# Sixteen gate tiles through seven-product units, weight sums by accumulating DMA, stores on SyncE

## The chip, the core and the metric

The kernel runs on one core of one Trainium2 chip. What counts is the device time of one execution in microseconds (us); lower is better. TensorE (PE) multiplies, VectorE (DVE) and ScalarE (ACT) work on tiles, GpSimd (POOL) and SyncE (SP) issue transfers here, and POOL does a few small operations too.

## The reference, cut to what matters

One residual block over 1024 tokens of width 1024, in float32:

```python
h   = rmsnorm(x, ln_mix)
z   = h @ w_in                      # q | k | v | g | pool channels u | gate_logits (2 x 1024)
y_ret  = (silu(g) * groupnorm(retention(q, k, v))) @ w_ret_up
y_pool = (multiscale_pool(u, pool_w) * pool_scale) @ w_pool_up
gates  = sigmoid(gate_logits + b_gate)
x   = x + (gates[..., :D] * y_ret + gates[..., D:] * y_pool) @ w_o
x   = x + square(relu(rmsnorm(x, ln_mlp) @ w_up)) @ w_down
out = rmsnorm(x, ln_final)
```

The change is about `gate_logits`, a 1024 x 1024 by 1024 x 2048 product, and about how the weights of `h2 @ w_up` are prepared.

## The kernel before

**Products.** A float32 operand is held as a pair of rounded halves, hi and lo, and each product is three passes (hi hi, hi lo, lo hi). The hi part is made by ACT (line 132), the lo part by DVE (line 133): that is `split_pair`. Everything is feature-major: a tile is 128 features by 1024 tokens, in two halves of 512 tokens, and a matmul has 128 x 128 stationary weights and 512 moving columns. A full tile, `feature_major`, has 8 blocks of the inner dimension x 3 passes x 2 halves = 48 matmuls.

**Stages.** q, k, v and the retention by heads; the swish gates `ps_g` (8 tiles); then 8 times a gate tile `ps_ga` and a tile of the retention's up-projection `ps_yr`; the pool channels; the gate tiles `ps_gb` (8 tiles); the pool's up-projection `ps_yp`; `ps_o`; then the MLP, `up` and down. Sixteen gate tiles take 16 x 48 = 768 matmuls. All of that stays in SBUF; only `x1` and the MLP's activations go to DRAM.

**Seven-product units.** The MLP's up-projection is done by a scheme of the Strassen-Winograd kind. A unit j takes a 2 x 2 block of weights (two feature tiles by two halves of the inner dimension: a11, a12, a21, a22) and the 2 x 2 blocks of the moving operand, and does seven block products of 12 matmuls each instead of eight: 84 matmuls for two feature tiles. It needs four sums of weight blocks, s1 = a21 + a22, s2 = s1 + a11, s3 = a11 + a21, s4 = a12 + s2. DVE adds them (lines 620, 621, 631 and 636), and all seven stationary operands are then split. The sums of the moving blocks (T1 to T4) are made once, in `moving_operands`.

**Buffers and queues.** The tag `w` has four buffers of 8 KB per partition: in the up stage each unit takes two of them, `raw` for its four weight blocks and `sums` for the four sums. The four output tiles of a unit, `o[0]` to `o[3]`, have one buffer each, since the moving operands fill the rest of tags `r` and `h`: the next unit cannot write its outputs before the store of the last ones has landed. SP issues the loads; POOL issues the stores of `x1` and of the activations. The order of instructions on each engine is set when the program is built, by a scheduler with a model of the engines; on the chip each queue then runs in that order, and an instruction whose wait isn't over holds up all that stand behind it on its queue.

Of the kernel before, what the change touches and what calls it, by code (L numbers as in the profile page):

```python
# [10 lines left out]
F32 = mybir.dt.float32  # L11
# [27 lines left out]
def block_kernel(ctx: ExitStack, tc: tile.TileContext, a: dict, out: bass.AP):  # L39
# [116 lines left out]
    def token_rstd(sums, name):  # L156
# [11 lines left out]
        return spread(rstd_of(ssq, name, n), n, name)  # L168

# [226 lines left out]
    retT = []  # L396
    for f in range(KT):
        w = load_piece(a["w_fm"][8 + f], f"w_g{f}")
        r = retn[f]
        pairs = []  # L400
        for half in range(2):
            sl = slice(half * HALF, (half + 1) * HALF)
            ps = mm_bank(f"ps_g{f}_{half}")
            feature_major(ps, w, hT, half)
            sig = mm_bank(f"sig{f}_{half}")
            nc.vector.tensor_tensor(ps, ps, R1[:, sl], ALU.mult)
            nc.scalar.activation(sig, ps, AF.Sigmoid)
            nc.vector.scalar_tensor_tensor(
                r[:, sl], r[:, sl], vec[:, V_GNG + f : V_GNG + f + 1], sig, ALU.mult, ALU.mult
            )  # L410
            nc.vector.tensor_tensor(r[:, sl], r[:, sl], ps, ALU.mult)
            dst = pair_tile("r", f"retT{f}_{half}")
            split_pair(dst, r[:, sl])
            pairs.append(dst)
        retT.append(pairs)


    mixed = []
    for f in range(KT):
        w = load_piece(a["w_fm"][20 + f], f"w_ga{f}")  # L420
        m = a_tile("a", f"m{f}")
        for half in range(2):
            sl = slice(half * HALF, (half + 1) * HALF)
            ps = mm_bank(f"ps_ga{f}_{half}")
            feature_major(ps, w, hT, half)
            nc.vector.tensor_tensor(ps, ps, R1[:, sl], ALU.mult)
            nc.scalar.activation(
                m[:, sl], ps, AF.Sigmoid,
                bias=vec[:, V_BG + f : V_BG + f + 1],
            )  # L430
        w = load_piece(a["w_ret"][f], f"w_ret{f}")
        for half in range(2):
            sl = slice(half * HALF, (half + 1) * HALF)
            ps = mm_bank(f"ps_yr{f}_{half}")
            feature_major(ps, w, retT, half)
            nc.vector.tensor_tensor(m[:, sl], m[:, sl], ps, ALU.mult)
        mixed.append(m)


# [3 lines left out]
    ypT = []  # L443
    pooled = []
    for g, win in enumerate(WINDOWS):
# [22 lines left out]
    sgB = []  # L468
    for f in range(KT):
        w = load_piece(a["w_fm"][28 + f], f"w_gb{f}")  # L470
        s = a_tile("r", f"sgB{f}")
        for half in range(2):
            sl = slice(half * HALF, (half + 1) * HALF)
            ps = mm_bank(f"ps_gb{f}_{half}")
            feature_major(ps, w, hT, half)
            nc.vector.tensor_tensor(ps, ps, R1[:, sl], ALU.mult)
            nc.scalar.activation(
                s[:, sl], ps, AF.Sigmoid,
                bias=vec[:, V_BG + KT + f : V_BG + KT + f + 1],
            )  # L480
        sgB.append(s)
        if f < 4:
            pairs = []
            for half in range(2):
                ps = aux_bank(f"ps_pw{f}_{half}")
                exact(
                    ps,
                    lambda s: pw[:, s, f * P : (f + 1) * P],
                    lambda s: pooled[f][half][:, s, :],
                )  # L490
                dst = pair_tile("r", f"ypT{f}_{half}")
                split_scaled(dst, ps, vec[:, V_PSC + f : V_PSC + f + 1])
                pairs.append(dst)
            ypT.append(pairs)


    mixT = []
    for f in range(KT):
        if f % 2 == 0:
            w = load_piece(a["w_pool"][f // 2], f"w_po{f}", cols=256)  # L500
        pairs = []
        for half in range(2):
            sl = slice(half * HALF, (half + 1) * HALF)
            ps = mm_bank(f"ps_yp{f}_{half}")
            feature_major(ps, w, ypT, half, nk=4, j0=(f % 2) * P)
            s, m = sgB[f], mixed[f]
            nc.vector.tensor_tensor(s[:, sl], s[:, sl], ps, ALU.mult)
            nc.vector.tensor_tensor(m[:, sl], m[:, sl], s[:, sl], ALU.add)
# [6 lines left out]
    dram = ctx.enter_context(tc.tile_pool(name="dram", bufs=1, space=bass.MemoryType.DRAM))  # L515
    x1_dram = dram.tile([KT, P, S], F32, name="x1_dram")
    act_dram = [dram.tile([NJ, P, 2, HALF], F32, name=f"act_dram{i}") for i in range(3)]
    act_dram.append(dram.tile([NJ, P, HALF], F32, name="act_dram3"))
# [11 lines left out]
    B11, B21, B22, T1, T2, T3, T4 = range(7)  # L530
# [21 lines left out]
    for k in range(4):  # L552
# [20 lines left out]
        for f in (k, k + 4):  # L573
            nc.gpsimd.dma_start(x1_dram[f], x1[f])
# [7 lines left out]
    def up(j):  # L582
        raw = w_tile(f"raw_up{j}", F32)
        nc.sync.dma_start(raw, a["w_up"][j])
        raw = raw.rearrange("p (b j) -> p b j", b=4)
        a11, a12, a22, a21 = (raw[:, i, :] for i in range(4))
# [327 lines left out]
```

## Time and profile before

| what | value |
|---|---|
| median of 3 runs | 1421.11 us (1419.1 to 1422.63) |
| profiled execution, its own time | 1419.43 us |
| its span, first to last instruction | 1417.7 us |
| PE busy | 1385.3 us, 98% of the span, 6656 matmuls |
| DVE busy | 891.6 us, 63% |
| ACT busy | 502.4 us, 35% |
| POOL busy | 65.6 us, 5% |
| DMA | 183.11 MB, 129 GB/s in the mean |

A busy share is an average over stages; what a stage is worth is read from its own stretch of the span. The view by windows gives for each stretch the busy time of each engine, the granted TensorE clock (1.00 is full), the share of the 16 DMA engines' time that was busy, and GB/s. The chain of waits follows the work that ended last back to its start, and names the engine that it was on at each step.

### The profile page before, as it was taken

The page shows a single profiled execution, that of the slowest core. Times are in us where ns is not written, and L with a number is a line of the kernel's source. Part 1 is how long each engine was busy: PE and PEld are TensorE (multiplying, and loading weights), DVE is VectorE, ACT ScalarE, POOL GpSimd, SP SyncE. Part 2 cuts the span into 40 slices and gives each one's busy share as a digit, 9 for nine tenths or more (in the row PEclk, how much of TensorE's full clock was granted, in tenths as well). Part 3 has the DMA queues.
Part 4 walks back from the last instruction along what each step waited for, and adds up shares of the span by engine and source line. Part 5 has one row for each costly group of instructions (what it writes and reads, how often), then busy time and mean ns, then how long its engine had stood idle before and what let it go on. Part 6 is the DMA issues. An engine that isn't in the chain of part 4 may idle for free.

```text
span 1417.7 us, 17117 instructions
## 1 busy us (share of the span) xinstructions
PE 1385.3 (98%) x6656; PEld 1162.8 (82%) x6656; DVE 891.6 (63%) x1461; ACT 502.4 (35%) x832; POOL 65.6 (5%) x107
## 2 busy tenths in 40 slices
PE   9999999999999999999999999999998999999985
PEld 6998999888888888888887788888887888878874
DVE  5766667763222246327558788777777867669593
ACT  6232324432111112223345343333333544435272
POOL 0000000000000000000000111110111000000001
PEclk9999999999999999999999999999999999999998
DMA  9112011012111211113322244434459977739251
GB/s 350 48 57 60 31 31 44 32 45 60 45 45 45 67 45 45 45 45 119 134 74 104 90 163 157 157 133 149 164 218 385 402 252 240 244 138 371 94 178 60
DMA packets 56209, 183.11 MB, mean 129 GB/s; under 512 B 6528, under 2 KB 8576, under 8 KB 54080
## 3 DMA queue, kind: packets, MB, share of 16 engines
q1 hardware_dynamic: 45408, 143.98, 29.4%
q0 software_dynamic: 10576, 38.02, 7.1%
q8 instruction: 52, 0.85, 0.2%
q14 instruction: 29, 0.24, 0.1%
q10 hardware_dynamic: 144, 0.03, 0.0%
HBM read 144.24 MB, written 37.75 MB: 128 GB/s over the span
## 4 chain that ended last, share of the span: by engine, by line
PE 94%; DVE 2%; issue 2%; ACT 1%; DMA 0%; POOL 0%; POOLq 0%; SPq 0%; DVEq 0%; ACTq 0%
PE ps_v L119 6%; PE ps_g L119 6%; PE ps_o L119 6%; PE ps_gb L119 6%; PE ps_yr L119 6%; PE ps_ga L119 6%; PE ps_dnX L716 6%; PE ps_upZ L598 6%; PE ps_upV L598 6%; PE ps_upX L598 6%; PE ps_dnV L716 6%; PE ps_dnZ L716 5%; PE ps_qT L119 3%; PE ps_kT L119 3%; PE ps_upY L598 3%; PE ps_dnY L716 3%
## 5 line engine op out<-in xcount | busy, mean ns | idle before, releaser
L716 PE MATMUL ps_dnX<-db,da 128*128 128x512 f32 x384 | 94.1, 394 | 4.3 <-ACT db L132 4.3
L119 PE MATMUL ps_v<-w_v_hi,hT 128*128 128x256 f32 x512 | 95.9, 284 | 0.0
L598 PE MATMUL ps_upX<-mv,a_up 128*128 128x512 f32 x384 | 94.2, 390 | 1.7 <-DVE a_up L133 1.6
L598 PE MATMUL ps_upZ<-mv,s_up 128*128 128x512 f32 x384 | 93.1, 390 | 0.3 <-ACT s_up L132 0.3
L119 PE MATMUL ps_g<-hT,w_g 128*128 128x512 f32 x384 | 90.2, 391 | 0.0
L716 PEld LDWEIGHTS ps_dnX<-db,da 128*128 128x128 f32 x384 | 73.0, 191 | 20.2 <-ACT db L132 4.7
L119 PE MATMUL ps_ga<-hT,w_ga 128*128 128x512 f32 x384 | 88.3, 389 | 0.0
L119 PE MATMUL ps_yr<-retT,w_ret 128*128 128x512 f32 x384 | 88.3, 389 | 0.0
L119 PE MATMUL ps_gb<-hT,w_gb 128*128 128x512 f32 x384 | 87.8, 389 | 0.0
L119 PE MATMUL ps_o<-mixT,w_o 128*128 128x512 f32 x384 | 87.5, 389 | 0.0
L598 PEld LDWEIGHTS ps_upX<-mv,a_up 128*128 128x128 f32 x384 | 71.9, 188 | 17.3 <-DVE a_up L133 2.0
L598 PEld LDWEIGHTS ps_upZ<-mv,s_up 128*128 128x128 f32 x384 | 71.9, 188 | 15.9 <-ACT s_up L132 1.1
L119 PEld LDWEIGHTS ps_ga<-hT,w_ga 128*128 128x128 f32 x384 | 72.1, 188 | 15.0
L119 PEld LDWEIGHTS ps_yr<-retT,w_ret 128*128 128x128 f32 x384 | 72.1, 188 | 15.0
L119 PEld LDWEIGHTS ps_gb<-hT,w_gb 128*128 128x128 f32 x384 | 72.1, 188 | 15.0
L119 PEld LDWEIGHTS ps_o<-mixT,w_o 128*128 128x128 f32 x384 | 72.0, 188 | 14.9
L119 PEld LDWEIGHTS ps_g<-hT,w_g 128*128 128x128 f32 x384 | 71.3, 188 | 14.2
L119 PEld LDWEIGHTS ps_v<-w_v_hi,hT 128*128 128x128 f32 x512 | 80.8, 192 | 0.0
L119 PE MATMUL ps_v<-w_v_lo,hT 128*128 128x256 f32 x256 | 72.7, 284 | 0.0
L613 ACT ACTIVATE act<-act 128x512 f32<-128x512 f32 x64 | 40.4, 632 | 69.0 <-DVE act L612 66.2
L132 ACT ACTIVATE s_up<-sum_up 128x512 fp32r<-128x512 f32 x64 | 39.9, 629 | 64.8 <-PE ps_upZ L598 24.7
L119 PE MATMUL ps_qT<-hT,w_qT 128*128 128x512 f32 x192 | 49.9, 407 | 1.8 <-ACT hT L136 1.5
(231 smaller groups left out, 2621.2 us busy)
## 6 DMA issues: line engine op xcount, KB each, us to landing
act_dram<-act POOLq DMA_DIRECT2D x48, 512.0 KB, 3.6
ad<-act_dram SPq DMA_DIRECT2D x48, 512.0 KB, 6.0
raw_up<-in_w_up_dram SPq DMA_DIRECT2D x16, 1024.0 KB, 4.9
wa_lo<-in_w_down_dram SPq DMA_DIRECT2D x16, 512.0 KB, 9.0
wb_hi<-in_w_down_dram SPq DMA_DIRECT2D x16, 512.0 KB, 4.1
wc_lo<-in_w_down_dram SPq DMA_DIRECT2D x16, 512.0 KB, 5.2
wc_hi<-in_w_down_dram SPq DMA_DIRECT2D x16, 512.0 KB, 5.8
xT<-in_xT_dram SPq DMA_DIRECT2D x8, 512.0 KB, 9.4
```

Source lines behind the costliest of these rows:

```text
L119: nc.tensor.matmul(ps, stationary(k, sa), moving(k, sb), start=i == 0, stop=i == n - 1)
L132: nc.scalar.activation(dst[:, 0, :], src, AF.Copy)
L598: nc.tensor.matmul(ps, w[:, sa, k * P : (k + 1) * P], h2[x][k][:, sb, :], start=start and k == 0 and n == 0, stop=k == 3 and n == 2, skip_ ...
L613: nc.scalar.activation(dst, dst, AF.Square)
L716: nc.tensor.matmul(banks[i][:, c0 : c0 + n], w[:, sa, i * P : (i + 1) * P], x[:, sb, c0 : c0 + n], start=start and j == 0 and m == 0, stop ...
```

## The change

Three things are done together.

1. The sixteen gate tiles go through eight units of seven products (`gates`), which share the code with the up-projection (`seven`). The moving blocks of the normalised input that the units need (T1 to T4) are made from a second load of x (`mixed_blocks`). Because these take 16 buffers of tag `r`, the retention output, the pool output and the sigmoids no longer stay in SBUF: each is stored to DRAM and loaded again. The order of stages becomes swish with the pool in between, gates, `ps_yp`, `ps_yr`, `ps_o`.
2. The sums of weight blocks are no longer added by DVE, in the gate units and in the up units alike. SP loads `raw` with three blocks (768 KB) and fills all four blocks of `sums` with a21 (1024 KB, one block read four times); then three accumulating transfers from POOL's queue add a22 to s1, s2 and s4 (768 KB), a11 to s2, s4 and s3 (768 KB), and a12 to s4 (256 KB). They write the same tile, so each waits until the one before it has landed.
3. The stores of `x1` and of the activations move from POOL's queue to SP's, among the loads.

```diff
+    def seven(name, src, moving, done):
+        src = src.rearrange("p (b j) -> p b j", b=4)
+        raw = w_tile(f"raw_{name}", F32).rearrange("p (b j) -> p b j", b=4)
+        nc.sync.dma_start(raw[:, :3, :], src[:, :3, :])
+        a11, a12, a22 = (raw[:, i, :] for i in range(3))
+        sums = w_tile(f"sum_{name}", F32).rearrange("p (b j) -> p b j", b=4)
+        s1, s2, s4, s3 = (sums[:, i, :] for i in range(4))
+        nc.sync.dma_start(sums, src[:, 3:, :].to_broadcast([P, 4, HALF]))
+        for b, i0, i1 in ((2, 0, 3), (0, 1, 4), (1, 2, 3)):
+            nc.gpsimd.dma_start(
+                sums[:, i0:i1, :], src[:, b : b + 1, :].to_broadcast([P, i1 - i0, HALF]),
+                accum_op=ALU.add,
+            )
+
+        def mult(ps, src, x, start=True):
+            w = pair_tile("a", f"w{x}_{name}")
+            split_pair(w, src)
...
+        mult(X, a11, B11)
+        nc.scalar.activation(p1, X, AF.Copy)
+        mult(Y, s2, T2)
+        nc.vector.tensor_tensor(u2, p1, Y, ALU.subtract)
+        mult(X, a12, B21, start=False)
+        done(0, 0, X)
+        mult(Z, s1, T1)
+        nc.vector.tensor_tensor(u4, u2, Z, ALU.add)
+        mult(V, s3, T3)
+        done(1, 1, V, u4)
+        mult(Z, s4, B22, start=False)
+        done(0, 1, Z, u2)
+        mult(V, a22, T4, start=False)
+        done(1, 0, V, u2)
...
-        w = load_piece(a["w_fm"][20 + f], f"w_ga{f}")
-        m = a_tile("a", f"m{f}")
-        for half in range(2):
-            sl = slice(half * HALF, (half + 1) * HALF)
-            ps = mm_bank(f"ps_ga{f}_{half}")
-            feature_major(ps, w, hT, half)
-            nc.vector.tensor_tensor(ps, ps, R1[:, sl], ALU.mult)
...
+    def mixed_blocks(k):
+        xw = w_tile(f"xw{k}", F32).rearrange("p (i t) -> p i t", i=2)
+        nc.gpsimd.dma_start(xw, a["xT"].rearrange("(i k p) t -> k p i t", i=2, p=P)[k])
...
+            nc.vector.tensor_tensor(dst, x, y, op)
+            hx[t][k] = pair_tile("r", f"hx{t}_{k}")
+            split_pair(hx[t][k], dst)
...
+    def gates(i):
...
+            nc.vector.tensor_tensor(y, y, R1[:, sl], ALU.mult)
+            nc.scalar.activation(
+                dst, y, AF.Sigmoid, scale=-1.0 if m else 1.0,
+                bias=vec[:, V_BG + f : V_BG + f + 1],
+            )
+            left[m] -= 1
+            if not left[m]:
+                nc.sync.dma_start(sg_dram[f], o[m])
+
+        seven(f"sg{i}", a["w_gate"][i], hx, done)
...
-            nc.gpsimd.dma_start(x1_dram[f], x1[f])
+            nc.sync.dma_start(x1_dram[f], x1[f])
...
-        nc.vector.tensor_tensor(s1, a21, a22, ALU.add)
-        nc.vector.tensor_tensor(s2, s1, a11, ALU.add)
...
-        nc.gpsimd.dma_start(act_dram[0][j], o[0])
-        nc.gpsimd.dma_start(act_dram[2][j], o[2])
...
+                nc.sync.dma_start(act_dram[0][j], o[0])
+                nc.sync.dma_start(act_dram[2][j], o[2])
```

**How the order moves, on POOL.** In the middle of the up stage POOL's queue held the four stores of each unit (units 6 and 7; `act3_6` is the output tile 3 of unit 6):

```order
L651 DMA act_dram1_5139<-act1_6_6694 128x1024
L645 DMA act_dram2_5140<-act2_6_6695 128x1024
L644 DMA act_dram0_5138<-act0_6_6693 128x1024
L652 DMA act_dram3_5141<-act3_6_6696 128x512
L651 DMA act_dram1_5139<-act1_7_6838 128x1024
```

It now holds nothing but the accumulating transfers, unit after unit (two of 768 KB, one of 256 KB):

```order
L187 DMA sum_up13_7977<-in_w_up_dram 128x512
L187 DMA sum_up14_8121<-in_w_up_dram 128x3x512 x2
L187 DMA sum_up14_8121<-in_w_up_dram 128x512
L187 DMA sum_up15_8265<-in_w_up_dram 128x3x512 x2
L187 DMA sum_up15_8265<-in_w_up_dram 128x512
```

The transfers of one unit stand in a chain on a queue that runs in order, so the sums of unit 15 cannot begin before the last of unit 14 has been issued.

**On SP.** Before, the up stage's part of SP's queue was one load per unit, and the unit's number is all that differs:

```order
L584 DMA raw_up8_6976<-in_w_up_dram 128x2048
L584 DMA raw_up9_7120<-in_w_up_dram 128x2048
L584 DMA raw_up10_7264<-in_w_up_dram 128x2048
L584 DMA raw_up11_7408<-in_w_up_dram 128x2048
L584 DMA raw_up12_7552<-in_w_up_dram 128x2048
```

Now two loads and four stores alternate:

```order
L181 DMA raw_up9_7399<-in_w_up_dram 128x1536
L185 DMA sum_up9_7401<-in_w_up_dram 128x4x512
L713 DMA act_dram2_5415<-act2_6_6965 128x1024
L712 DMA act_dram0_5413<-act0_6_6963 128x1024
L716 DMA act_dram1_5414<-act1_6_6964 128x1024
L717 DMA act_dram3_5416<-act3_6_6966 128x512
L181 DMA raw_up10_7543<-in_w_up_dram 128x1536
L185 DMA sum_up10_7545<-in_w_up_dram 128x4x512
```

The loads of unit 9 need the two `w` buffers of unit 7, and the stores of unit 6 stand behind them.

**On DVE.** The additions are gone, and the splits of unit 9 (`w4` is s2, `w3` is s1, `w5` is s3, `w2` is s4) stand among the evacuations of unit 8. Before, at the same place for units 11 to 14, the sums were added nearly three units ahead of their use:

```order
L620 TENSOR_TENSOR sum_up14_7842<-raw_up14_7840 128x512
L631 TENSOR_TENSOR sum_up14_7842<-raw_up14_7840 128x512
L648 TENSOR_TENSOR act1_11_7414<-tmp_up11_7411,ps_upV11_7420 128x512
L621 TENSOR_TENSOR sum_up14_7842<-sum_up14_7842,raw_up14_7840 128x512
L641 TENSOR_TENSOR act1_11_7414<-act0_11_7413,act2_11_7415 128x512
L133 TENSOR_TENSOR a11_up13_7709<-raw_up13_7696,a11_up13_7709 128x512
```

Now:

```order
L133 TENSOR_TENSOR w4_up9_7428<-sum_up9_7401,w4_up9_7428 128x512
L715 TENSOR_TENSOR act3_7_7110<-act0_7_7107,act1_7_7108 128x512
L211 TENSOR_TENSOR tmp_up8_7262<-tmp_up8_7262,ps_Yup8_7265 128x512
L133 TENSOR_TENSOR w1_up9_7444<-raw_up9_7399,w1_up9_7444 128x512
L215 TENSOR_TENSOR u4_up8_7263<-tmp_up8_7262,ps_Zup8_7266 128x512
L133 TENSOR_TENSOR w3_up9_7461<-sum_up9_7401,w3_up9_7461 128x512
```

The split of s2 of unit 9 stands ahead of the reading of the bank Y of unit 8: if the sums of unit 9 are late by then, DVE stops, and the banks of unit 8 are not read.

More of the change, by code (lines that the diff above doesn't have):

```diff
@@ L442, in block_kernel, with pool @@
     split_pair(pw, pw_raw)
[L443 removed]
+    yp_dram = dram_tile("yp_dram", (4, P, S))
     pooled = []
[L445 removed]
+    def pool(g):
+        win = WINDOWS[g]
         w = load_piece(a["w_fm"][16 + g], f"w_pu{g}")
@@ L498, in block_kernel @@
+    for i in range(KT):
+        gates(i)
+    ypT = []
+    for f in range(4):
+        y = a_tile("a", f"ypf{f}")
+        nc.sync.dma_start(y, yp_dram[f])
+        ypT.append([])
+        for half in range(2):
+            dst = pair_tile("h", f"ypT{f}_{half}")
+            split_pair(dst, y[:, half * HALF : (half + 1) * HALF])
+            ypT[f].append(dst)
+    mixed = []
     for f in range(KT):
```

245 lines of the change are left out of this document (125 added, 120 removed).

## The prediction

> **What bounds the kernel now.** I read the page first (span, busy times, the chain of waits by engine), then the windows by stage, then the chain in order of time.
>
> ```profile
> span 1417.7 us, 17117 instructions
> PE 1385.3 (98%) x6656; PEld 1162.8 (82%) x6656; DVE 891.6 (63%) x1461; ACT 502.4 (35%) x832; POOL 65.6 (5%) x107
> PE 94%; DVE 2%; issue 2%; ACT 1%; DMA 0%; POOL 0%; POOLq 0%; SPq 0%; DVEq 0%; ACTq 0%
> ```
>
> The chain that ended last lies on PE for 94%. By stage (columns: window, length, then busy time and count for PE, PEld, DVE, ACT, POOL, then the granted clock, the share of the DMA engines, GB/s):
>
> ```profile
> 278.00:500.00 222.00, 222.00 (x981) 183.82 (x980) 74.44 (x92) 43.89 (x58) 0.77 (x1) 1.00 0.16 49
> 545.00:637.00 92.00, 92.00 (x408) 76.17 (x407) 33.39 (x43) 23.44 (x33) 0.00 (x0) 1.00 0.14 46
> 762.00:805.00 43.00, 39.03 (x176) 30.84 (x175) 36.70 (x61) 20.69 (x36) 5.36 (x4) 1.00 0.28 98
> 805.00:1060.00 255.00, 255.00 (x1127) 211.22 (x1126) 199.26 (x323) 98.36 (x162) 29.98 (x56) 1.00 0.44 163
> 1060.00:1084.00 24.00, 19.71 (x88) 16.02 (x87) 13.96 (x23) 5.43 (x9) 4.00 (x8) 1.00 0.98 358
> 1100.00:1125.00 25.00, 25.00 (x112) 20.68 (x111) 22.95 (x39) 14.51 (x26) 0.00 (x0) 1.00 1.03 404
> 1125.00:1225.00 100.00, 100.00 (x443) 82.80 (x442) 69.28 (x111) 44.00 (x78) 0.00 (x0) 1.00 0.77 259
> ```
>
> In the gate stages (rows 1 and 2) and in the up stage (row 4) PE is never idle. The idle time lies at the start of the up stage (row 3, 4.0 us) and at its end (row 5, 4.3 us). So a matmul taken away is worth its whole time there, and a DVE instruction taken away is worth nothing. The reader should also see the DMA column: 0.14 to 0.16 in the gate stages, 0.44 in the up stage, and at most 1.03, which moved 404 GB/s.
>
> **The matmuls removed.** The chain in order of time gives their pace (start, length, what):
>
> ```profile
> 348.82 10.88 PE ps_ga L119 x48
> 593.62 43.52 PE ps_gb L119 x192
> 899.99 2.72 PE ps_upV L598 x12
> ```
>
> 48 matmuls in 10.88 us are 226.7 ns each, the same in all three rows; a block product of 12 is 2.72 us. Sixteen gate tiles of 48 matmuls become eight units of 84: 768 - 672 = 96 fewer, 96 x 226.7 ns = **21.8 us**. This is the only gain on the path. The up stage keeps its 84 per unit, 7 x 2.72 = 19.04 us.
>
> **DVE and ACT.**
>
> ```profile
> L426 DVE TENSOR_TENSOR ps_ga<-ps_ga,R x16: 699/700/700, 332.5 to 490.3; 128x512 f32<-128x512 f32 x16
> L133 DVE TENSOR_TENSOR s_up<-sum_up,s_up x64: 679/683/694, 771.8 to 1055.7; 128x512 fp32r<-128x512 f32 x64
> L132 ACT ACTIVATE s_up<-sum_up x64: 614/632/636, 767.4 to 1055.1; 128x512 fp32r<-128x512 f32 x64
> ```
>
> A gate unit has seven splits, three additions and four multiplications by R1 on DVE: 14 x 0.69 = 9.7 us in 19.04; ACT has seven hi parts, a copy and four sigmoids, 12 x 0.65 = 7.8 us. An up unit loses four additions, 2.7 us of DVE, which lie beside a PE that is busy throughout: nothing. The moving blocks for the gates cost 4 x 8 x 0.69 = 22 us of DVE during swish and pool. These stages have 12 tiles of 10.88 us, 131 us in all; their DVE work was 72 us in the 105 us around swish (with the end of the retention) and 31 us in the 50 us around the pool (rows below), and about 11 us of retention splits leave: 114 in 131 or more, a share of 0.87 at worst. The up stage ran at 199/255 = 0.78 without a gap, so I put 1 us on it and no more.
>
> ```profile
> 225.00:330.00 105.00, 105.00 (x526) 89.02 (x525) 71.92 (x126) 40.74 (x68) 2.19 (x2) 1.00 0.14 46
> ...
> 500.00:525.00 25.00, 25.00 (x112) 20.68 (x111) 11.11 (x16) 4.34 (x5) 0.00 (x0) 1.00 0.14 43
> 525.00:550.00 25.00, 25.00 (x112) 20.70 (x111) 19.72 (x29) 4.44 (x6) 0.00 (x0) 1.00 0.20 59
> ```
>
> **The accumulating transfers** decide the rest, and the trace before has none. The rows that come nearest (operations x count, KB each, median us from issue to landing):
>
> ```profile
> raw_up<-in_w_up_dram SPq DMA_DIRECT2D x16, 1024.0 KB, 4.9
> pw_raw<-in_pool_w_dram POOLq DMA_DIRECT2D x1, 256.0 KB, 3.2
> act_dram<-act POOLq DMA_DIRECT2D x48, 512.0 KB, 3.6
> raw_w_ga<-in_w_fm_dram SPq DMA_DIRECT2D x8, 512.0 KB, 3.5
> wc_hi<-in_w_down_dram SPq DMA_DIRECT2D x16, 512.0 KB, 5.8
> ```
>
> From 256 KB at 3.2 to 1024 KB at 4.9 a further 768 KB costs 1.7 us, and what is fixed is 3.2 - 0.6 = 2.6. Three estimates for a unit's chain of 768, 768 and 256 KB, each after the landing of the last:
> - as plain loads: 4.3 + 4.3 + 3.2 = 11.8 us;
> - the data counted twice (source and destination are both read), the fixed part once: 6.0 + 6.0 + 3.8 = 15.8;
> - as two whole transfers, a read and a write: 23.6.
>
> POOL's queue takes the chains one after another, so a chain longer than 19.04 us sets the pace instead of PE. The first two are shorter, the third is not. I take the middle one: the sum must have both operands, and within one transfer the fixed part need not be paid twice.
>
> Then contention. An up unit moved 1024 KB in and 1792 KB out; it will load 768 + 1024, accumulate 1792 and store 1792: 5376 KB, 5.5 MB. At the up row's 163 GB/s for a share of 0.44, 5.5 MB in 19.04 us (289 GB/s) is a share of 0.78, and with the accumulated data counted twice 385 GB/s, or 1.04: just what the fullest row showed. In the row with 0.77 the 512 KB load `wc_hi` landed in 5.8 us against 3.5 for `raw_w_ga` at 0.16. The plain traffic of a unit, 3584 KB at 2.3 us per MB above the fixed part, is 8 us; the chain leaves 3 x 2.6 = 7.8 us in which it moves no data itself. If 40% of the plain traffic still falls into the chain's data, it is 15.8 + 3.2 = **19.0 us**: it just fits. Bounds: 11.8 if plain and unhindered, 23.6 + 8 = 32 at worst. In a gate unit the stores are 1024 KB, so the chain is nearer to 18.5.
>
> The sentence for the skill: the Trainium skill, "Collectives: The Full Stack", section "The bandwidth ceiling: the fold count and why AG ≠ RS ≠ AR", says that an adding transfer costs two source reads on the same ring and so moves at half the rate; no run so far shows it here, and by it the chain is at least the middle estimate. The Trainium skill, "DMA: Bandwidth & Descriptors", section "Anatomy of one DMA — SWDGE (gpsimd) path", gives about 2.0 us plus bytes at 436 GB/s, an estimate of 10.2 us for the chain, by which the whole 21.8 us would stay; its 2.6 us for 256 KB is under the measured 3.2.
>
> **Slack.** The loads for unit j+3 go out when the last split of unit j+1 frees its buffer, some 15 us into unit j. Before, SP waited in the same manner:
>
> ```profile
> SPq L584 <- DVE s_up L133: 250.5, 14, 20.1
> ```
>
> They land about 6.6 us later (4.9 for the first MB, 1.7 for the next 768 KB), two accumulations follow (12 us), so s2 is there 34 us after the start of unit j. DVE splits it ahead of the bank Y of unit j+2, which it can read as late as 6 us into that unit, 44 us after the start of unit j. So 10 us of lateness can be used up in each stage before PE waits, and a chain of 19.5 us costs nothing over 16 units. At the start of each stage there is less: the second unit's sums can only be loaded when the last `w_o` buffers come free, at the end of `ps_o`. That start cost 4.0 us before, on R2 and the first splits; I put 3 us more on the two starts together, and 1 us on the reloads of the pool and retention outputs at the end of the gates, which have the 43.5 us of `ps_yp` to arrive in.
>
> **The stores on SP** stand behind loads that wait. The outputs have one buffer each, and the wait for a store is already there:
>
> ```profile
>   DVE act L634: 4.2, 2
> ```
>
> 4.2 us in 2 waits (of all that waited for the stores of the activations). While the splits are early, SP's wait is over before the stores are ready, and a store from SP costs what one from POOL did (3.6 us to landing, above): nothing. If SP's loads come late, the stores do too.
>
> **Sum.** 1419.4 (the profiled execution: span 1417.7 and 1.7 around it) - 21.8 + 1 + 3 + 1 = 1402.6. That execution is 1.7 under the median of the runs, so the median should be **1404 us**.
>
> **Rivals.**
> 1. *The chain overruns and sets the pace.* One mechanism: POOL's queue, three serial transfers per unit, in the up stage above all. For it: 1.04 of the DMA engines with data counted twice, and `wc_hi` at 5.8 us. Against: the fixed parts leave room. At 22 us a chain: up 16 x 3.0 - 10 = 37, gates 8 x 2 - 10 = 6, so 1404 + 43 = 1447. It decides from 20.9 us on: 16 x 1.9 - 10 = 20, which with the starts eats the gain. The skill's rule of two reads, cited above, points this way.
> 2. *A draw*: the chain at 20.5 (1.5 x 16 - 10 = 14), or stores that SP holds back by 1 us in each of 16 units while DVE waits on the single output buffers; 1404 + 14 to 16 = 1419.
> 3. *The boundaries*: sums of the first units, `ps_yp` and `ps_yr` waiting on reloads, each 3 or 4 us that now follow one another: 1404 + 9 = 1413. For it: row 3 and row 5 show that stage changes are where PE idles. Against: SP's loads of 512 KB land in 3.5 us, far within `ps_yp`.
> 4. *That the change doesn't do what it says*, the matmuls not being fewer: the counts exclude it, 6656 should be 6560.
>
> **How the numbers follow.** Forecast 0.43 (1398 to 1409), rival 3 0.10, rival 2 0.12, rival 1 0.35. A measurement of this kernel tells a change from none from about 0.3% on, 4 us. Forecast and rival 3 are faster: 0.53. The draw is within 4 us: 0.12. Rival 1 is slower: 0.35. Below, the range takes in chains as short as plain loads with the start's old idle time gone: 1404 - 5 - 4 = 1395. Above it reaches to rival 1 at 22 us and a little over, 1450; a chain as slow as two whole transfers lies beyond it.
>
> **What would show it.** PE's count must be 6560, and the gate units in the windows must come every 19.04 us. Right: PE at full busy time in the middle of the up stage, accumulations of 768 KB landing in 6 to 7 us, POOL waiting for SP's loads rather than for its own transfers. Wrong: landings of 8 us and more, POOL always waiting for its own last transfer, PE waiting for splits of the sums by a constant amount in every up unit, and a DMA share near 1.0 there. If PE waits instead for a load of `yp`, `ret` or `sg`, it is rival 3; if DVE waits for the stores, rival 2. The forecast is wrong if the up stage's mean pace is over 20 us per unit.

## The result, and the profile after

The changed kernel takes 1542.91 us (median of 4 runs, 1539.95 to 1544.28); the kernel before took 1420.11 beside it. The ratio is 1.0859, 95% interval 1.0837 to 1.0882: slower by 123 us, where 1404 us and a gain of 16 were forecast, and outside the range of 1395 to 1450.

The page of the changed kernel (span; busy times; one DMA queue, POOL's; the chain by engine):

```profile
span 1538.2 us, 17516 instructions
PE 1407.1 (91%) x6560; PEld 1167.6 (76%) x6560; DVE 912.7 (59%) x1509; ACT 536.7 (35%) x912; POOL 113.7 (7%) x115
q0 software_dynamic: 25552, 54.79, 19.2%
PE 20%; DVE 2%; ACT 1%; issue 0%; POOLq 0%; POOL 0%; DVEq 0%; ACTq 0%
```

PE has its 96 matmuls fewer, and yet it is busy for 22 us longer (1407 against 1385) in a span that is 120 us longer. The chain of waits was on PE for 94% before; now it can be followed for only about a quarter of the span. The windows of the middle of the gate units and of the middle of the up stage (the second is the same stretch that the prediction showed of before):

```profile
400.00:525.00 125.00, 107.14 (x433) 86.09 (x432) 49.95 (x79) 35.21 (x59) 18.60 (x16) 0.90 0.88 208
805.00:1060.00 255.00, 214.16 (x856) 170.71 (x855) 133.84 (x213) 72.91 (x128) 37.43 (x32) 0.91 0.88 218
```

In the up stage 856 matmuls are 10.19 units of 84, so a unit takes 25.0 us and not 19.04. Of the 6.0 us too much, 4.0 are idle time of PE (255 - 214.2 over 10.19 units). The other 2.0 are matmuls at a lower clock: 856 at 226.7 ns are 194 us, and they took 214, at a granted clock of 0.91. A gate unit takes 24.3 us. The DMA share rose from 0.44 to 0.88 and the bytes only from 163 to 218 GB/s.

PE's waits and POOL's (us in total, times, longest):

```profile
PE ps_Zup L197 <- DVE u_up L215: 55.5, 14, 6.8
PE ps_Zsg L197 <- DVE u_sg L215: 19.2, 5, 6.6
PE ps_Ysg L197 <- ACT w_sg L132: 14.2, 2, 13.6
PE spread_b L151 <- POOL rstd_b L145: 7.5, 1, 7.5
...
POOL sum_up L187 <- DMA sum_up<-in_w_up_dram: 327.9, 34, 13.2
POOL sum_sg L187 <- DMA sum_sg<-in_w_gate_dram: 144.3, 18, 12.0
```

One wait in nearly every unit: the second product into bank Z waits for DVE to read the first (`u_up`, line 215). DVE reads it late because a split of the next unit's sums stands ahead of it and waits for the transfers: the row below is such a split (`w_up` from `sum_up`), which waited 11.3 us for ACT's half of it, which waits for the sums. POOL's queue shows for which transfers (start, length, instructions, idle time before):

```profile
1046.41 0.69 DVE L133 TENSOR_TENSOR w_up<-sum_up,w_up 128x512 fp32r<-128x512 f32 x1 [11.29 <-ACT w_up L132]
1019.55 2.20 POOL L187 DMA_DIRECT2D sum_up<-in_w_up_dram  x2 [12.42 <-DMA sum_up<-in_w_up_dram]
1032.06 1.28 POOL L187 DMA_DIRECT2D sum_up<-in_w_up_dram  x1 [10.30 <-DMA sum_up<-in_w_up_dram]
1045.97 2.20 POOL L187 DMA_DIRECT2D sum_up<-in_w_up_dram  x2 [12.64 <-DMA sum_up<-in_w_up_dram]
```

The `x2` is the 256 KB accumulation of one unit with the first 768 KB one of the next, the `x1` the second 768 KB one. So this period of 26.4 us (12.5 + 13.9) is two accumulations of 768 KB in series, and POOL does little but wait for its own last transfer. The 256 KB run beside the first 768 KB of the next unit and add nothing to it. PE's instructions around the second of these, in order of time:

```profile
1035.86 2.88 PE L197 MATMUL ps_Zup<-mv,w_up 128*128 128x512 f32 x12
1049.56 5.18 PE L197 MATMUL ps_Zup<-mv,w_up 128*128 128x512 f32 x12 [5.38 <-DVE u_up L215]
```

After 5.4 us of idle time the same twelve matmuls take 5.18 us instead of 2.88: a stall is paid nearly one and a half times. The landings:

```profile
sum_up<-in_w_up_dram POOLq DMA_DIRECT2D x32, 768.0 KB, 11.6
sum_up<-in_w_up_dram SPq DMA_DIRECT2D x16, 1024.0 KB, 8.8
raw_up<-in_w_up_dram SPq DMA_DIRECT2D x16, 768.0 KB, 7.0
sum_up<-in_w_up_dram POOLq DMA_DIRECT2D x16, 256.0 KB, 4.2
act_dram<-act SPq DMA_DIRECT2D x48, 512.0 KB, 6.9
```

### The profile page after: what moved, and what is told of

It is laid out like the page before. It is cut to its first block, busy times and chain, and to the rows that moved or that the text cites. A ratio compares the mean times of both kernels' runs of the same rounds, so it can differ in the third digit from the quotient of the medians.

```text
span 1538.2 us, 17516 instructions
## 1 busy us (share of the span) xinstructions
PE 1407.1 (91%) x6560; PEld 1167.6 (76%) x6560; DVE 912.7 (59%) x1509; ACT 536.7 (35%) x912; POOL 113.7 (7%) x115
## 3 DMA queue, kind: packets, MB, share of 16 engines
q0 software_dynamic: 25552, 54.79, 19.2%
## 5 line engine op out<-in xcount | busy, mean ns | idle before, releaser
L197 PE MATMUL ps_Zup<-mv,w_up 128*128 128x512 f32 x384 | 117.9, 465 | 55.8 <-DVE u_up L215 55.5
L197 PEld LDWEIGHTS ps_Zup<-mv,w_up 128*128 128x128 f32 x384 | 87.1, 231 | 82.1 <-DVE u_up L215 61.4
L133 DVE TENSOR_TENSOR w_up<-sum_up,w_up 128x512 fp32r<-128x512 f32 x64 | 43.7, 687 | 136.0 <-ACT w_up L132 135.1
L197 PE MATMUL ps_Xup<-mv,w_up 128*128 128x512 f32 x384 | 98.7, 400 | 0.5 <-DVE w_up L133 0.5
L197 PE MATMUL ps_Vup<-mv,w_up 128*128 128x512 f32 x384 | 93.5, 390 | 3.2 <-DVE act L706 3.0
L132 ACT ACTIVATE w_up<-sum_up 128x512 fp32r<-128x512 f32 x64 | 38.1, 618 | 152.8 <-DMA sum_up<-in_w_up_dram 97.2
L783 PEld LDWEIGHTS ps_dnX<-db,da 128*128 128x128 f32 x384 | 73.1, 191 | 20.1 <-ACT db L132 4.7
L197 PEld LDWEIGHTS ps_Xup<-mv,w_up 128*128 128x128 f32 x384 | 74.5, 195 | 17.7 <-DVE w_up L133 1.2
L197 PEld LDWEIGHTS ps_Vup<-mv,w_up 128*128 128x128 f32 x384 | 71.8, 188 | 19.4 <-DVE act L706 4.4
L187 POOL DMA_DIRECT2D sum_up<-in_w_up_dram x48 | 55.6, 1216 | 402.4 <-DMA sum_up<-in_w_up_dram 327.9
L119 PEld LDWEIGHTS ps_o<-mixT,w_o 128*128 128x128 f32 x384 | 72.0, 188 | 14.9
L133 DVE TENSOR_TENSOR w_sg<-sum_sg,w_sg 128x512 fp32r<-128x512 f32 x32 | 21.9, 687 | 80.6 <-ACT w_sg L132 80.1
## 6 DMA issues: line engine op xcount, KB each, us to landing
sum_up<-in_w_up_dram POOLq DMA_DIRECT2D x32, 768.0 KB, 11.6
```

The lines of the kernel that those rows point to most:

```text
L119: nc.tensor.matmul(ps, stationary(k, sa), moving(k, sb), start=i == 0, stop=i == n - 1)
L132: nc.scalar.activation(dst[:, 0, :], src, AF.Copy)
L133: nc.vector.tensor_tensor(dst[:, 1, :], src, dst[:, 0, :].bitcast(F32), ALU.subtract)
L187: nc.gpsimd.dma_start(sums[:, i0:i1, :], src[:, b : b + 1, :].to_broadcast([P, i1 - i0, HALF]), accum_op=ALU.add,)
L197: nc.tensor.matmul(ps, w[:, sa, k * P : (k + 1) * P], moving[x][k][:, sb, :], start=start and k == 0 and n == 0, stop=k == 3 and n == 2, s ...
L783: nc.tensor.matmul(banks[i][:, c0 : c0 + n], w[:, sa, i * P : (i + 1) * P], x[:, sb, c0 : c0 + n], start=start and j == 0 and m == 0, stop ...
```

## The experiments

**The sums back on DVE.** The gates by seven products and the stores on SP stay; `raw` is loaded whole and DVE adds, as before the change.

```diff
-        nc.sync.dma_start(raw[:, :3, :], src[:, :3, :])
+        nc.sync.dma_start(raw, src)
-        nc.sync.dma_start(sums, src[:, 3:, :].to_broadcast([P, 4, HALF]))
-        for b, i0, i1 in ((2, 0, 3), (0, 1, 4), (1, 2, 3)):
-            nc.gpsimd.dma_start(
...
+        nc.vector.tensor_tensor(s1, a21, a22, ALU.add)
+        nc.vector.tensor_tensor(s2, s1, a11, ALU.add)
...
+        nc.vector.tensor_tensor(s3, a11, a21, ALU.add)
...
+        nc.vector.tensor_tensor(s4, a12, s2, ALU.add)
```

> The gates through seven products and the stores on SP stay; the sums are added by DVE again, in the gate units and in the up units, and the weights of a unit are loaded in one transfer of 1024 KB. Theory A (the serial accumulations set the pace of both stages): without them PE's pace of 19.04 us per unit returns and the whole 21.8 us of fewer matmuls shows, 1400 to 1405 us. Theory B (the other parts cost too: the stores that now stand behind loads on SP, or the reloads of sigmoids, pool and retention outputs): some of the 122 us stays, 1425 us or more, and PE waits in the up stage for DVE that waits for stores.

1406.86 us, 2 above the first theory's range; ratio to before 0.9904 (0.9881 to 0.9927). The accumulating transfers, with the loads that they need, cost 136 us; the other two parts are a gain of 13. Of the 21.8 us, 9 were still missing. Some 6 of them lie where the gates start (the window from 370 to 380 us, PE's wait there, and the load that stands in the chain of waits ahead of it):

```profile
PE 1368.3 (97%) x6560; PEld 1146.9 (82%) x6560; DVE 969.7 (69%) x1605; ACT 546.5 (39%) x912; POOL 32.0 (2%) x43
370.00:380.00 10.00, 6.30 (x17) 4.22 (x16) 8.85 (x16) 4.06 (x8) 0.00 (x0) 0.66 0.48 155
400.00:525.00 125.00, 125.00 (x553) 103.52 (x552) 78.42 (x121) 48.13 (x76) 0.00 (x0) 1.00 0.30 112
805.00:1060.00 255.00, 255.00 (x1127) 211.15 (x1126) 194.81 (x315) 95.28 (x156) 0.00 (x0) 1.00 0.44 163
PE ps_Ysg L191 <- ACT w_sg L132: 2.5, 1, 2.5
359.56 6.77 DMA raw_sg<-in_w_gate_dram
```

In the middle of both stages PE is never idle (19.0 us per unit). At 370 to 380 us PE does 17 matmuls in 10 us, 27 fewer than at full pace, while DVE is busy for 8.85 of them. The weights of the first gate unit are on the chain too: their load went out only at 359.6 us, when DVE's split of a moving block (`hx`) had freed the `w` buffer that it needed.

**The same transfers without adding.** The sums are left out; bytes, waits and queues stay. (POOL's queue then moves its 54.79 MB in 14800 packets, not the 25552 of the changed kernel.)

```diff
-                accum_op=ALU.add,
```

> The changed kernel with plain copies in place of the accumulating transfers: same queue, same sizes, same rows of 2 KB, same chain of three, nothing added (the sums are wrong, so the values of the gates and of the MLP are too; the work is the same). Theory A1 (it is the adding that makes a transfer long: two operands are read, so its data take twice as long): 768 KB land in 5 to 6 us instead of 11.6, the two serial ones of a unit are under 19 us, and the time is 1400 to 1410 us. Theory A2 (it is the chain itself, transfers from POOL with 384 rows each, or the 1.28 us that POOL takes to issue one): landings stay over 9 us, and the time stays over 1480 us. Theory C (the DMA engines are full with the plain traffic): in between, DMA share near 0.9 and landings of 8 us, 1440 us.

1460.47 us: 82 us of the 136 go with the adding, 54 with transfers that only copy. None of the three expected times is met; the third theory comes nearest, with a share of 0.86 and landings of 8.3 us. The window of 900 to 1090 us and POOL's 768 KB:

```profile
900.00:1090.00 190.00, 177.84 (x762) 145.47 (x761) 113.70 (x180) 62.28 (x108) 18.58 (x27) 0.97 0.86 266
sum_up<-in_w_up_dram POOLq DMA_DIRECT2D x32, 768.0 KB, 8.3
```

A unit takes 20.9 us (762/84 in 190), 0.86 x 20.9 = 18.0 us of it work of the DMA engines. So a unit is over PE's 19.04 us here although that work is not.

**The transfers alone.** A kernel with transfers only: chains of six transfers of each kind, and one chain beside a stream of 1 MB loads and stores on SP.

> None of the block's work, only transfers: six serial ones each, from POOL, of 768 KB plain, 768 KB accumulating (one block read three times, rows of 2 KB), 768 KB accumulating from rows of 6 KB, 256 KB accumulating, 256 KB plain; from SP 768 KB plain; and six accumulations of 768 KB beside a stream of loads and stores of 1 MB on SP. Theory A1: 768 KB plain 4.3 us from issue to landing, accumulating 6.5 to 7.5 alone and 11 to 13 beside the stream; 256 KB accumulating about 4. Theory A2 (a fixed cost per transfer or per row in POOL): plain and accumulating alike, 8 us or more alone. A theory in which an accumulation is slow by itself, each row waiting for its own read: 11 us alone, and no longer beside the stream.

Landings (`accwide` adds 768 KB that are read once, in rows of 6 KB), and the windows of the chains (plain 768 KB, accumulating 768 KB, accumulating 256 KB, plain 256 KB, accumulating beside the stream; five transfers lie in each of the first four; the last three columns are clock, DMA share, GB/s):

```profile
plain<-in_w_up_dram POOLq DMA_DIRECT2D x6, 768.0 KB, 6.6
acc<-in_w_up_dram POOLq DMA_DIRECT2D x6, 768.0 KB, 7.6
accwide<-in_w_up_dram POOLq DMA_DIRECT2D x6, 768.0 KB, 6.8
spplain<-in_w_up_dram SPq DMA_DIRECT2D x6, 768.0 KB, 6.2
accbeside<-in_w_up_dram POOLq DMA_DIRECT2D x6, 768.0 KB, 16.5
accsmall<-in_w_up_dram POOLq DMA_DIRECT2D x6, 256.0 KB, 4.0
plainsmall<-in_w_up_dram POOLq DMA_DIRECT2D x6, 256.0 KB, 3.4
```

```profile
10.00:44.00 34.00, 0.00 (x0) 3.81 (x5) 1.00 0.58 114
54.00:92.00 38.00, 0.00 (x0) 6.31 (x5) 1.00 0.64 100
143.00:164.00 21.00, 0.00 (x0) 4.24 (x5) 1.00 0.40 62
169.00:186.00 17.00, 0.00 (x0) 2.71 (x5) 1.00 0.21 72
245.00:312.00 67.00, 2.27 (x12) 5.04 (x4) 1.00 1.04 370
```

The first theory met 7.6 and 4.0 nearly, but not the plain 6.6 (4.3 expected) nor the 16.5 (11 to 13).

Two things follow. The form and the adding are each dear. One block of 256 KB read three times takes 6.6 us as a plain load, from SP 6.2, while `raw_up` with its 768 KB read once landed in 4.4 us in the kernel of the next paragraph (from SP, not alone). Adding 768 KB read once takes 6.8, and both together take 7.6, less than the two surcharges added up. Whether the form is dear for the repeated reading or for its short rows of 2 KB, no run separates. And the rest is company: the same accumulation lands in 7.6 us alone, 11.6 in the changed kernel, 16.5 beside the stream.

The windows also price the work of the DMA engines, as share times time: a plain 768 KB is 0.58 x 34/5 = 3.9 us, an accumulating one 4.9, 256 KB 0.7 and 1.7. With 8.4 us for the 2816 KB of a unit of DVE sums (0.44 x 19.04), an up unit of the change adds up to 2 x 4.9 + 1.7 + 5.2 (1024 KB read four times, at 3.9 per 768) + 7.6 (2560 KB) = 24.3 us. Its own trace says 25.0 x 0.88 = 22.0. Either is more than the 19.04 us in which PE could do the unit, and at the fullest share seen here, 1.04, even 22.0 us of work take 21.2. The prices do not add up exactly (with plain copies they give 21.3 us, and that trace said 18.0), so that no arrangement of the transfers keeps up with PE is likely, not shown.

The Trainium skill's rule that the add of a collective's ReduceScatter needs two source reads and so runs at half the rate ("Collectives: The Full Stack", section "The bandwidth ceiling: the fold count and why AG ≠ RS ≠ AR"), carried over to these transfers within one core, has the trace on its side for one block of 256 KB (work 1.7 against 0.7) and against it for the 768 KB (4.9 against 3.9).

**Two small accumulations.** s1 and s3 get one independent transfer of 256 KB each, s2 and s4 are added by DVE; SP loads 768 KB, and a21 into two blocks only.

```diff
+        nc.sync.dma_start(sums[:, :2, :], src[:, 3:, :].to_broadcast([P, 2, HALF]))
+        for b, i0 in ((2, 0), (0, 1)):
+            nc.gpsimd.dma_start(sums[:, i0, :], src[:, b, :], accum_op=ALU.add)
```

> Accumulation kept, but small and without a chain: s1 = a21 + a22 and s3 = a21 + a11 by one transfer of 256 KB each, independent of each other; DVE adds s2 and s4. Theory A: two transfers of 4 to 5 us per unit on POOL are far below 19.04 us, so PE sets the pace again and the time is that of the kernel with all sums on DVE, 1400 to 1406 us. If accumulation does harm by its mere presence (a blocked port of DVE, or POOL's issue), 1430 us or more.

1431.2 us, ratio to before 1.008 (1.006 to 1.0101): slower than before, though by under 1%, and 24 us behind the kernel of DVE sums, where nothing was expected by the first theory. Some 9 of the 24 lie in the up stage (321 us from its first product to its last, against 312), 8 at the start of the gates and in them, 5 in `ps_o`; which wait makes each stays open. The DMA share is 0.64, so this is not the engines' work. DVE shows a wait that the kernel of DVE sums has not got (and SP's 768 KB, read once, their landing):

```profile
DVE sum_up L207 <- DMA sum_up<-in_w_up_dram: 65.3, 16, 8.2
```

```profile
raw_up<-in_w_up_dram SPq DMA_DIRECT2D x16, 768.0 KB, 4.4
```

**One accumulation of 768 KB, the rest on DVE.** Only the first of the three transfers stays; loads as in the change.

```diff
-        for b, i0, i1 in ((2, 0, 3), (0, 1, 4), (1, 2, 3)):
+        for b, i0, i1 in ((2, 0, 3),):
+        nc.vector.tensor_tensor(s2, s2, a11, ALU.add)
...
+        nc.vector.tensor_tensor(s3, s3, a11, ALU.add)
...
+        nc.vector.tensor_tensor(s4, s4, a11, ALU.add)
+        nc.vector.tensor_tensor(s4, s4, a12, ALU.add)
```

> The changed kernel with only the first of its three accumulating transfers (768 KB, into three sums); the second and third are replaced by four additions on DVE in place. Nothing else moves: SyncE still loads 768 KB and the 1024 KB broadcast. POOL's queue now has one transfer of 8 to 12 us per unit, under the 19.04 us of the matmuls. Theory A, POOL's serial chain alone sets the pace of 26 us: with the chain under 19.04 the pace is that of the matmuls, 1405 to 1415 us. Theory B, the time from a buffer's release to its finished sums counts beside it (in the kernel of two small accumulations some 15 us of landings in series already cost 24 us): here raw 6, broadcast 8, accumulation 10, some 24 us in series, so 1435 to 1470 us with POOL waiting for SyncE's loads and not for its own transfers.

1510.5 us, worse than both theories, with a DMA share of 0.63 between 805 and 1060 us and one accumulation of 8.2 us per unit. One period, on DVE, SP and POOL in turn:

```profile
995.64 0.69 DVE L217 TENSOR_TENSOR sum_up<-sum_up,raw_up 128x512 f32<-128x512 f32 x1 [5.01 <-DMA sum_up<-in_w_up_dram]
1003.81 0.69 DVE L210 TENSOR_TENSOR sum_up<-sum_up,raw_up 128x512 f32<-128x512 f32 x1 [2.67 <-DMA sum_up<-in_w_up_dram]
...
986.30 0.33 SPq L181 DMA_DIRECT2D raw_up<-in_w_up_dram  x1
987.64 0.38 SPq L185 DMA_DIRECT2D sum_up<-in_w_up_dram  x1
1009.93 0.33 SPq L181 DMA_DIRECT2D raw_up<-in_w_up_dram  x1
...
996.16 1.29 POOL L187 DMA_DIRECT2D sum_up<-in_w_up_dram  x1 [23.66 <-DMA sum_up<-in_w_up_dram]
```

The broadcast goes out at 987.6 and has landed at 995.6, where DVE takes it at once and POOL starts to add; that has landed at 1003.8, where DVE takes it at once; 6 us later the next loads go out. That DVE takes them at once is the order of its list, set by the scheduler, which in this kernel puts the additions of a unit two ahead right behind the split that frees its buffer, and ahead of the read of bank Z that PE waits for (the `raw` tiles of three units in succession, 4, 5 and 6, are 6703, 6849 and 6995; `w_up_6824` and `u_up_6709` belong to unit 4, `sum_up_6997` to unit 6):

```
870 L133 TENSOR_TENSOR w_up_6824<-raw_up_6703,w_up_6824 128x512
874 L217 TENSOR_TENSOR sum_up_6997<-sum_up_6997,raw_up_6995 128x512
883 L210 TENSOR_TENSOR sum_up_6997<-sum_up_6997,raw_up_6995 128x512
888 L216 TENSOR_TENSOR u_up_6709<-tmp_up_6708,ps_Zup_6712 128x512
```

So in this kernel there is one set of loads under way at a time, not two, and the unit takes the loop's 24 us: from release to landed broadcast 9.3, adding 8.2, and DVE to the next release 6.

**Two loads and no accumulation.** The loads of the kernel of two small accumulations, everything added by DVE.

> The kernel of DVE sums (1406.9 us), with its weight load of 1024 KB cut in two as in the kernel of two small accumulations (768 KB, and the fourth block broadcast into two sums, 512 KB), but with no accumulating transfer: all four sums are added on DVE in place. Theory of the loop: the time of a unit cannot be under (from the load's issue to ready operands) + (about 5 us of DVE until the next release), because DVE's list has the additions of unit j+2 right behind the split that frees its buffers. With one accumulation in between that was about 15 + 5 = 20 us (measured pace 20.1), with one of 768 KB 18 + 6 = 24 (measured 24); here 6 to 7 + 5 = 12, far under 19.04, so 1404 to 1411 us. Rival, the added broadcast traffic or the second load on SyncE itself is what cost 24 us in the kernel of two small accumulations: 1420 to 1432 us.

```profile
850.00:1040.00 190.00, 190.00 (x840) 157.34 (x839) 148.34 (x242) 71.65 (x120) 0.00 (x0) 1.00 0.49 171
```

1412.61 us, with PE busy for 190.00 of 190 us in the middle of the up stage; 1.6 us over the expected range, in part from a longer wait at the gates' start (4.9 us on `w_sg`, 2.5 with the load in one). With some 6 us from release to landing in place of 15, the loop fits, so the extra broadcast was not what cost the 24 us. The pace of 20.1 us in that expectation is that of the whole stage; from 850 to 1050 us it was 19.3.

**Accumulation in the gates alone.** The up units add on DVE.

> The changed kernel with accumulating transfers in the eight gate units only; the 16 up units load 1024 KB at once and add on DVE. Theory: the loss lies in each stage by itself, 45 us in the gates (573 - 376 = 197 us for 152.3 of matmuls) and 87 us in the up stage, so 1407 + 45 - 4 (what the gates of the DVE kernel lose at their start anyway) = 1448 us, range 1440 to 1456, with the up stage at 311 to 314 us. Rival: the up stage is hindered by something else that the change brings (stores on SyncE, the shape of the seven-product helper), and stays over 330 us: 1470 us and more.

1444.0 us, within the expected range: the gates cost 37 us, the up stage with its start the other 99. Without accumulation the up stage is free of it (PE waits for split weights there for 1.9 us in all). The losses lie in each stage by itself.

**The stores back on POOL**, in the kernel of DVE sums:

```diff
-                nc.sync.dma_start(act_dram[0][j], o[0])
+                nc.gpsimd.dma_start(act_dram[0][j], o[0])
...
```

> The kernel of DVE sums (seven-product gates, all sums on DVE, 1406.9 us), with the stores of x1 and of the activations moved back from SyncE to POOL. This is the third part of the change alone, read backwards. Theory: the stores cost the same from either queue as long as SyncE's loads are early, so 1404 to 1410 us, with 512 KB of activations landing in about 3.6 us from POOL as before the change (2.8 from SyncE). Rival: in the changed kernel SyncE's wait for stores delays weight loads, so that with POOL the up stage gets back its 1.5 us and more: below 1403 us. Other rival: POOL's issue costs time that DVE sees: over 1412 us.

1407.31 us (ratio 0.9913, 0.9894 to 0.9931) against 1406.86: in that kernel the third part of the change is worth nothing either way.

**A pause in POOL's chain.** The changed kernel, with a slow operation on 16 columns between the first and the second accumulation of each up unit.

```diff
+            if b == 0 and name[:2] == "up":
+                nc.gpsimd.tensor_tensor(pause, sums[:, 1, :16], two, ALU.pow)
```

> The changed kernel (1542.9 us) with one small, slow instruction on POOL in each up unit between the first and the second accumulation (a power of 16 columns of one sum, about 3 to 5 us, call it d; its result is not used). No transfer is added. Theory, POOL's chain of two accumulations of 768 KB in series sets the pace of 26 us: each up unit becomes longer by 0.7 to 1.0 d (a little may come back as less contention), so for d = 4 the time goes up by 45 to 65 us, to 1588 to 1608. Rival, the loop over two sets of buffers sets it: a unit takes half of what lies between a release and the release two units later, so at most d/2 per unit, 32 us; and if POOL stands idle between the units, nothing: 1543 to 1575 us.

1549.0 us, 6 us more. The pause was 2.9 us in each of 16 units, 47 in all. The operation, the landing and the window of 900 to 1160 us, and then the same window of the changed kernel:

```profile
L190 POOL TENSOR_TENSOR pause<-sum_up,two x16: 2924/2929/3392, 787.7 to 1165.8; 128x16 f32<-128x16 f32 x16
sum_up<-in_w_up_dram POOLq DMA_DIRECT2D x32, 768.0 KB, 10.5
900.00:1160.00 260.00, 214.74 (x836) 172.46 (x837) 130.04 (x205) 69.92 (x122) 65.37 (x40) 0.89 0.86 215
```

```profile
900.00:1160.00 260.00, 214.10 (x839) 171.88 (x838) 129.25 (x205) 69.94 (x123) 34.87 (x31) 0.89 0.86 217
```

Both do ten units in 260 us. So the chain's landings are not fixed lengths that add up to the pace: with the pause the accumulations land sooner (10.5 against 11.6 us), and so do SP's 768 KB (6.1 against 7.0). That it is the pause that lets SP's transfers get done is my reading, not shown. My theory of the chain, in the form in which I had put it down, falls.

**A megabyte more per unit**, copied within device memory, which nothing waits for; in the changed kernel, and as a control in that of DVE sums.

```diff
+        if j:
+            for i in (0, 2):
+                nc.sync.dma_start(echo[i // 2, j], act_dram[i][j - 1])
```

> The changed kernel (1542.9 us) with two more transfers per up unit on SyncE, from unit 1 on: two stored activation blocks of the unit before, 512 KB each, are copied within device memory to a place that nothing reads. They touch no tile and nothing waits for them. Theory, the work of the DMA engines sets the pace: a unit takes 26.4 us at a DMA share of 0.85, 22 us of work, while the kernel with the 3 us pause on POOL kept that pace and that share; 1 MB more is at least 2.6 us of work (at the 404 GB/s that the fullest window moved), twice that if reading and writing both count, so a unit becomes 3 to 6 us longer and the kernel 45 to 90 us: 1588 to 1633. Rival, the pace is set by waits in series (POOL's transfers, the release of buffers) while the DMA engines have 15% to spare, some 4 us per unit: 1543 to 1560 us, with the DMA share rising to 0.95 or more.

> The same copies added to the kernel of DVE sums (1406.9 us), as the control: there the DMA share of the up stage is 0.43, so 3 to 6 us of work more per unit (share 0.57 to 0.73) find room and cost nothing: 1405 to 1414 us. Rival, the copies cost through SyncE's queue (they stand ahead of the next weight load), whatever the DMA engines have to spare: over 1420 us, and then the same amount has to be taken off the other run.

The control took 1410.6 us, as expected. The changed kernel took 1533.8: not 45 to 90 us more but 9 less. Its window of 900 to 1150 us:

```profile
900.00:1150.00 250.00, 204.70 (x843) 164.47 (x841) 123.38 (x196) 67.92 (x119) 34.59 (x30) 0.90 0.97 266
```

A unit takes 24.9 us at a share of 0.97. So in the changed kernel the DMA engines had some 10% to spare, and their work alone isn't what makes 25 or 26 us. The scheduler also put the instructions of this kernel in another order (POOL's list now often has the first accumulation of a unit ahead of the last of the unit before), so the 9 us are not the effect of the copies alone.

What stands is two limits above PE's 19.04, close together: the work of the DMA engines, 22 us, and waits in series (landings stretched by company, splits in a fixed order, two sets of buffers), which with that work make 25 to 26. The waits show by themselves with one accumulation, where a unit of 24 us had a DMA share of 0.63; the work was never run without them. How landings, splits and buffers share the last 3 to 4 us per unit stays open.

**The blocks of the gates earlier**, in the kernel of DVE sums:

```diff
-        if f in (2, 4, 5, 6):
+        if f in (1, 2, 4, 5):
```

> The kernel of DVE sums (1406.9 us) with the combined moving blocks of the gates made after swish tiles 1, 2, 4 and 5 and not 2, 4, 5 and 6. Theory: of the 21.8 us of matmuls some 8 are lost where the gates start, because DVE is busy 85 to 88% between 350 and 400 us and the first gate unit's split of s2 and the last T2 come late; with the last blocks one swish tile (10.9 us) earlier and the work spread over 44 us more, 3 to 7 us of it come back: 1400 to 1404 us, 0.986 to 0.989 of the kernel before. Rival: the start waits on the weights of the first gate unit, not on the blocks: 1406 to 1408 us. Other rival: the earlier blocks fall into the end of the retention, where DVE is at 68%, and delay it: over 1409 us.

1400.28 us (1399.46 to 1404.76), ratio 0.9865 (0.9844 to 0.9887): the fastest version here, 20 us under before and 143 under the change. All four blocks come one or two tiles earlier.

```profile
PE 1363.8 (98%) x6560; PEld 1143.1 (82%) x6560; DVE 969.6 (69%) x1605; ACT 546.0 (39%) x912; POOL 32.3 (2%) x43
370.00:380.00 10.00, 9.60 (x42) 7.59 (x42) 9.97 (x18) 4.00 (x8) 0.00 (x0) 1.00 0.18 60
```

DVE is busier in this window than before (9.97 against 8.85 us), and PE loses almost nothing. So DVE's load in this window is not what costs PE. What is left is what stands in DVE's list ahead of the first gate unit's splits, and the load of that unit's weights, which goes out at 357.3 in place of 359.6 us; how much each gives stays open.

## Why the prediction was wrong

- **The matmuls removed, 21.8 us: right.** 6560 of them. The last kernel gets 20.1 of the 21.8 us (1420.4 - 1400.3).
- **The accumulating chain, "15.8 + 3.2 = 19.0 us: it just fits": this is the step that failed**, in both terms and in its method. The bare chain measures 7.6 + 7.6 + 4.0 = 19.2 us, not 15.8; as plain loads it is 16.6 and not 11.8. I had taken "a further 768 KB costs 1.7 us" from a load that reads each row once, and these read one block three times. The method had the three transfers one after another on POOL's queue; the trace has the 256 KB beside the next unit's first 768, so the queue's pace is two large accumulations, some 16 us bare (8.0 to 8.1 each from issue to issue, alone). That would have fitted. The contention, 3.2 us, was the larger miss: 4.0 us for each of the two by the median landings (11.6 - 7.6), and some 10 us in the period shown (26.4 - 16).
- **The DMA engines' work.** The shares of 0.78 to 1.04 that I worked out for a unit of 19.04 us are 14.9 to 19.8 us of work; it is 22.0. Bytes per second were the wrong measure: in the changed kernel's up stage a share of 0.88 moves 218 GB/s, in the fullest window of before 1.03 moved 404. This sum, at measured prices, would have warned without any theory of chains that the change could hardly run at PE's pace. The Trainium skill's figure for one transfer ("DMA: Bandwidth & Descriptors", section "Anatomy of one DMA — SWDGE (gpsimd) path") made the chain 10.2 us, an estimate for this case; the measured 16.6 us without adding decides against it.
- **Rival 1** came true, at 0.35. With the measured paces its own formula gives 16 x (25.0 - 19.04) - 10 = 85 and 8 x (24.3 - 19.04) - 10 = 32, so 1404 + 117 = 1521. The other 22 us lie in the starts and in the 10 us of slack that it took off in each stage, which no run separates. Its mechanism, POOL's serial queue, is only part of it, as the pause shows. Its price of 22 us a chain, which set the range's upper end, was too low; my bound of 32 was not carried into the range.
- **Slack, 10 us per stage:** an overrun of 6 us per unit uses it up in two units; right or wrong, it is worth 20 us at most of the 139 by which the forecast missed. The loads' 6.6 us to landing, on which it rests, were 8.8.
- **DVE beside PE, 1 us: right in the middle of the stages** (125.00 and 255.00 us full with the sums on DVE). A gate unit has five additions on DVE, not three, which changes nothing there. But the moving blocks, "a share of 0.87 at worst", cost some 6 us where the gates start: a mean over 131 us hid that the last of them stood, in DVE's list and in a `w` buffer, ahead of the first gate unit's weights. Making the blocks earlier brought it back.
- **The starts, 3 us:** PE waited 13.6 us for the first gate unit's sums alone, and 7.5 us at the start of the up stage for `rstd_b` (2.0 before).
- **The stores on SP, nothing: right** with the sums on DVE (1407.3 against 1406.9); in the changed kernel, where SP's loads come late, it was not tried.
- **What would show it** did: landings far over 8 us, POOL waiting for its own last transfer, PE waiting in nearly every unit, a pace of 25 us. A DMA share "near 1.0" was 0.88.

## What to carry to other kernels

Before work is moved from an engine with room to the DMA queues, add up the DMA engines' busy time per unit at the price of the very access pattern, measured alone, and compare it with the unit's time on the bounding engine; bytes over a peak rate say too little. A transfer that is put between a buffer's release and its first use lengthens a loop, and an engine's list in fixed order may stop on it two units ahead of where the data is needed. Where a gain falls short by a few microseconds, look at the stretch before the stage, not at its mean.

## What was not expected of the hardware

- Reading one block of 256 KB three times, in rows of 2 KB, is slow as a plain load too: 6.2 to 6.6 us for 768 KB, against 4.4 for 768 KB read once in rows of 6 KB.
- Adding costs 1.0 us of the DMA engines' work whether 256 or 768 KB are added (1.7 against 0.7, 4.9 against 3.9), but the same transfer of 768 KB lands in 7.6, 11.6 or 16.5 us according to what runs beside it.
- A pause of 2.9 us per unit in a saturated queue cost 0.4 us per unit, and 1 MB more per unit cost nothing (in another order of instructions).
- After a stall of 5.4 us PE's next twelve matmuls took 5.18 us in place of 2.88. After one of only 2.4 us, in the kernel with one accumulation, they took 4.51.
